# Loading the second query block of a prompt attention with the first, and a sample group's memory scores three side steps later

## The chip, the cores and the metric

The kernel runs on one core of one Trainium2 chip. The metric is the device time of one execution in microseconds; the median of the runs counts. The engines are named as in the profile: PE (TensorE), ACT (ScalarE), DVE (VectorE), POOL (GpSimd), and SP, whose queue issues most of the DMAs.

## What is computed

One layer of a hybrid decoder trunk, for a prompt (1 x 2048 tokens of 1024) and for a sample group (8 sequences of 4 new tokens, each with 8192 past tokens in a paged cache). One projection gives the inputs of four head groups: a convolution module, a pooling mixer, a stick-breaking attention (8 heads of 64) and a cross-attention into 256 memory tokens (4 heads of 128). Every group's output is multiplied by its own gate; all are concatenated, projected with `w_out`, normalised and added to the residual. The two parts that matter here:

```
def sb_block(q, k, v, bias, q_pos, k_pos):              # stick-breaking attention
    z = einsum('nqhd,nkhd->nhqk', q, k) * (64 ** -0.5) + bias
    mask = k_pos < q_pos
    log_1m = where(mask, log_sigmoid(-z), 0.0)
    rc = cumsum(log_1m, axis=3, reverse=True)
    a = exp(where(mask, log_sigmoid(z) + rc - log_1m, -inf))
    return einsum('nhqk,nkhd->nqhd', a, v)

def mem_attend(q, mk, mv):                              # cross-attention into the memory
    s = einsum('nqhd,nmhd->nhqm', q, mk) * (128 ** -0.5)
    return einsum('nhqm,nmhd->nqhd', softmax(s), mv)
```

## The kernel before

The program has three stages that follow each other on the engines.

The first is the projection of prompt and sample tokens, column group by column group. PE runs its products, and beside them the sample group's attention over the paged cache (`sample_all`) advances by steps that a rate sets. When its last step is through, its buffers are closed, the pool `sbr` of the prompt attention is opened in their place, and the first query block is loaded at once (`load(0, 0)`), while the last two column groups of the projection still run. Their results go to scratch in DRAM (`gsd`, `gcd`, `mixd`, `ydw`) through SP's queue.

The second stage is the prompt's stick-breaking attention, `sb_prompt`. It runs over 4 head pairs `hp` and 4 query blocks `qb` of 512 tokens each; within a block over key blocks `kc` from `qb` down to 0, and there over the two heads `hh` and two halves `q2` of the queries. I call one such step a pair, because it treats two tiles of 128 queries, and number the pairs from 1: block (0, 0) has pairs 1 to 4, block (0, 1) has the diagonal pairs 5 to 8 and the full pairs 9 to 12, and block (0, 2) begins with pair 13. `score` multiplies queries (`Q`) and keys (`kT`) into the PSUM tile `S` (two buffers); ACT makes two sigmoids of it, `gam` and `be`; DVE runs a product scan over `gam` into `E`; POOL multiplies `be` by `E`. Some steps later `turn` transposes `be` on PE into `AT` (two PSUM buffers) and copies it to `at`, and `values` multiplies it with `V` into `av`.

At the start of each block the loads of the next one are issued, if they have not been before:

```
            if bi + 1 < len(blocks) and blocks[bi + 1] not in loaded:
                loaded[blocks[bi + 1]] = load(*blocks[bi + 1])
```

A load of a block is eight DMAs, four of keys and four of queries (two heads, two halves of the partitions); the first block of a head pair also loads the values `V`. There are buffers for four `Q` tiles, two blocks.

Beside the attention a generator of side work, `side_work`, advances by one step each time the attention's cost has grown by `PACE` (4.0), from the ninth of its own steps on (`SLATE`). A full pair costs 2.66, a diagonal one 1.0 or 2.33. The side work is, in order: the sample group's memory attention (`sample_mem`), the rest of its stick-breaking attention (`sample_end`), the first output weights, and, once head pair 3 reports its first blocks, the first output parts and the convolution's second half. `sample_mem` loads eight tiles of transposed memory keys (`mkbT`, 512 KB each), then in two halves multiplies four of them with the sample queries into `smS`, which takes one of the two `AT` buffers, and adds them up in `smsc` on DVE. After each half it loads four tiles of memory values (`mvb`) into the key tiles' buffers. Then come the maximum `smx` on DVE, the exponential `smp` on ACT, which needs another activation table than the sigmoids, transposes, products with the values (`smO`) and the gate.

The third stage multiplies the mixed groups with `w_out` and normalises.

The order of PE's instructions is the order in which the code issues them. The other engines' orders, SP's queue among them, are set by a scheduler from the program; each engine then works through its own order, waiting where it must.

Of the kernel before, what the change touches and what calls it, by code (L numbers as in the profile page):

```python
# [37 lines left out]
K4 = 4  # L38
PACE = 4.0
SLATE = 8  # L40
LEAD = 2
LPACE = 3
AHEAD = 4
# [43 lines left out]
def kernel(  # L87
# [1043 lines left out]
    def sample_mem(sm, ps_, S):  # L1131
# [18 lines left out]
        def load(b):  # L1150
            t = sm.tile([P, 2, 512], F32, tag="mkb", name=f"mvb{b}", bufs=8)
            sp.dma_start(t, cmv[b].rearrange("(t p) c -> p t c", p=P))
            return t

        kT = []
        for b in range(NB):
            kT.append(sm.tile([P, 4, NMEM], F32, tag="mkb", name=f"mkbT{b}", bufs=8))
            sp.dma_start(kT[b], mkTd[b])
        vb = {}
        for k in range(2):  # L1160
            yield
            S = ps_(f"smS{k}")
            for b in range(4 * k, 4 * k + 4):
                for h in range(4):
                    pe.matmul(S[32 * h : 32 * h + 32, :NMEM], lhsT=qm[:, b, h, :], rhs=kT[b][:, h, :], start=b == 4 * k,
                              stop=b == 4 * k + 3, tile_position=(0, 32 * h))
            if k:
                dve.tensor_tensor(out=sc, in0=sc, in1=S[:, :NMEM], op=ALU.add)
            else:
                dve.tensor_copy(sc, S[:, :NMEM])  # L1170
            for b in range(4 * k, 4 * k + 4):
                vb[b] = load(b)
# [52 lines left out]
    def sb_loader(sbr):  # L1225

        KT, V = {}, {}

        def load(hp, qb):
            tok = slice(512 * qb, 512 * qb + 512)  # L1230
            Q = []
            for hh in range(2):
                pr = slice(64 * hh, 64 * hh + 64)
                kt = sbr.tile([P, 512], F32R, tag="kT", name=f"kT{hp}_{qb}_{hh}", bufs=10)
                qt_ = sbr.tile([P, 2, 512], F32R, tag="Q", name=f"Q{hp}_{qb}_{hh}", bufs=4)
                for x in range(2):
                    hx = slice(64 * x, 64 * x + 64)
                    sp.dma_start(kt[hx].bitcast(F32), kd[hp, pr, x, tok])
                    sp.dma_start(qt_[hx].bitcast(F32), qd[hp, pr, :, tok])
                KT[hp, hh, qb] = kt  # L1240
                Q.append(qt_)
            if qb == 0:
                V[hp] = sbr.tile([P, 16, P], F32, tag="V", name=f"V{hp}", bufs=2)
                sp.dma_start(V[hp], vd[:, P * hp : P * (hp + 1)].rearrange("(t p) c -> p t c", p=P))
            return Q, KT, V[hp]

        return load
# [336 lines left out]
    def out_weights(prod, pool_, eng, lead=1, raw=lambda j: "opm", lag=1):  # L1584


        ts = {}
        for j in range(lead):
            if j:
                yield  # L1590
            ts[j] = weight_load(prod, j, raw(j))
        for j in range(8 + lag):
            yield
            if 0 < j < 9:
                weight_high(prod, j - 1, ts[j - 1], pool_)
            if j >= lag:
                weight_low(prod, j - lag, ts.pop(j - lag), eng)
            if j < 8:
                weight_sum(prod, j, ts[j])
            if j + lead < 8:  # L1600
                ts[j + lead] = weight_load(prod, j + lead, raw(j + lead))
# [63 lines left out]
    def out_high(x):  # L1665
        prod, i, h = x
        rows = P if i < LAST else NS
        mh, ml = [opm.tile([P, 4, P], F32R, tag=n, name=f"{n}{prod}_{i}_{h}", bufs=2 * LEAD) for n in ("mh", "ml")]
        act.copy(mh[:, :, :rows], raws[x])  # L1669
# [145 lines left out]
    def main():  # L1815
        yield from z_groups(0, GROUPS[0][4:12])
        tasks.add(later_stats())
        yield from z_groups(0, GROUPS[0][12:14])
        tasks.add(sample_keys())
        yield from z_groups(0, GROUPS[0][14:])  # L1820
        tasks.add(state_rows(0))
        yield from z_groups(1, GROUPS[1][:-2])
        tasks.add(state_rows(1))
        yield from z_groups(1, GROUPS[1][-2:])
# [4 lines left out]
    due, blk = 0.0, {}  # L1829
    sbr = bx = None  # L1830
    for cost in main():
        tasks.step()
        due += rate * cost
        while sample is not None and due >= 1.0:
            due -= 1.0
            try:
                next(sample)
            except StopIteration:
                sample = None
                sx.close()  # L1840
                bx = ExitStack()
                sbr = bx.enter_context(tc.tile_pool(name="sbr", bufs=1, side="right", reuse_waits="tile"))
                load = sb_loader(sbr)
                blk[0, 0] = load(0, 0)
    tasks.drain()
    zx.close()

# [20 lines left out]
    last_ *= 2  # L1868
    lead_ = parts[: 2 * LEAD]
    raws, mix, accs, keep, stores = {}, {}, {}, {}, []  # L1870
# [3 lines left out]
    def side_work():  # L1874
        nonlocal opm, conv
        for i, part in enumerate((sample_mem, sample_end)):
            with tc.tile_pool(name=f"sm{i}", bufs=1, side="left", reuse_waits="tile") as sm2:
                yield from part(sm2, side_ps, S)
        opm = ox.enter_context(tc.tile_pool(name="opm", bufs=1, side="left", reuse_waits="tile"))
        yield from out_weights(1, opm, pool)  # L1880
        while (3, 0) not in flags:
            yield
        for x in lead_:
            out_load(x)
            out_combine(x)
            out_high(x)
            out_low(x, pool)
            yield

        while (3, 1) not in flags:  # L1890
            yield
        for x in parts[2 * LEAD : 2 * LEAD + 3]:
            out_load(x)
        cp = cx.enter_context(tc.tile_pool(name="cp", bufs=1, side="left", reuse_waits="tile"))
        conv = conv_post(cp, lambda n: conv_ps[0](n), lambda: cx.enter_context(
            tc.tile_pool(name="cpw", bufs=1, side="left", reuse_waits="tile")))
        while "centered" not in flags:
            next(conv)
            yield
# [30 lines left out]
    for cost in sb_prompt(load, blk, sb, bps, ops, flags):  # L1930
        steps += 1
        if steps > SLATE:
            due += cost
# [31 lines left out]
    def weights_after():  # L1965
# [4 lines left out]
        def spread(gen, start, step):  # L1970
            yield start
            for k, _ in enumerate(gen):
                yield start + step * k

        yield 2 * LEAD
        wr = lambda j: "wr"
        yield from spread(out_weights(7, op, dve, 1, wr), 2 * LEAD, 1.5)
        yield from spread(out_weights(2, opm, dve, 2, wr), at((7, 0, 0)) + 1, 1.4)
# [49 lines left out]

    ready = {d: set(lead_ if d < 3 else parts[: 2 * LEAD + 3]) for d in (3, 1, 0, -1)}
    for n, x in enumerate(parts):  # L2030
# [64 lines left out]
```

## Time and profile before

| | us |
|---|---|
| median of 3 runs | 2420.67 |
| the runs | 2415.16, 2420.67, 2429.53 |
| the profiled execution | 2418.47 |
| its span, first to last instruction | 2416.7 |
| PE busy in it | 2285.6 (95%) |
| DVE, POOL, ACT busy | 1718.3, 1306.8, 1117.5 |
| projection ends (last product begins) | 1490.28 |
| first product of the prompt attention | 1492.15 |
| first and last load of queries issued | 1475.53, 1874.9 |

Times within the profile count from the start of the span. A row of an engine gives the start, the time that the group of instructions took, and in brackets how long the engine had been idle and what ended that. The granted clock is that of TensorE, 1.00 being full speed.

### The profile page before, as it was taken

What the parts mean: (1) busy time and instruction counts of PE and PEld (TensorE: products, weight loads), DVE (VectorE), ACT (ScalarE), POOL (GpSimd) and SP (SyncE); (2) the same over time, 40 slices, a digit from 0 to 9 for tenths busy, and PEclk for the clock granted to TensorE, in tenths of its full rate; (3) what the DMA queues carried; (4) which work ended last, traced back from release to release, by engine and by line L of the source; (5) the groups of instructions that cost most, each with busy time, mean ns of one, the idle gap of its engine ahead of it and who ended that gap; (6) DMA issues with size and microseconds to landing.
All of it is one profiled execution on the core that took longest, in us unless ns stands there. A gap on an engine that the chain in (4) does not pass through costs nothing. (4 is left out here: it accounts for less than half of the span.)

```text
span 2416.7 us, 42137 instructions
## 1 busy us (share of the span) xinstructions
PE 2285.6 (95%) x15962; PEld 1774.5 (73%) x15962; DVE 1718.3 (71%) x2410; ACT 1117.5 (46%) x1939; POOL 1306.8 (54%) x1333
## 2 busy tenths in 40 slices
PE   7999999999999999999999998899999998989897
PEld 6998978898888777777777776455555556768775
DVE  5333774959757664587877777879798846687998
ACT  5322343242442322124242434788989954443554
POOL 2554544556574555655556564667877755453430
PEclk9999999999999999999999999999999999999998
DMA  5789988887778899987887767834333227887764
GB/s 179 223 260 298 348 290 287 284 272 263 263 254 292 277 344 325 323 287 262 275 270 269 262 218 179 239 79 117 89 88 79 64 64 242 266 272 254 245 234 170
DMA packets 340437, 562.14 MB, mean 233 GB/s; under 512 B 28481, under 2 KB 212929, under 8 KB 323834
## 3 DMA queue, kind: packets, MB, share of 16 engines
q1 hardware_dynamic: 284858, 290.72, 39.2%
q0 software_dynamic: 55376, 268.72, 31.3%
q8 instruction: 126, 2.06, 0.3%
q14 instruction: 77, 0.63, 0.1%
HBM read 469.28 MB, written 90.68 MB: 232 GB/s over the span
## 5 line engine op out<-in xcount | busy, mean ns | idle before, releaser
L959 DVE STREAM_TRANSPOSE T<-kt 128x1024 f32<-128x1024 f32 x256 | 308.9, 1226 | 183.4 <-PE sSA L972 177.2
L926 POOL DMA_INDIRECT vt<-in_cache_v_dram,idv x256 | 251.6, 983 | 242.1 <-PE sO L1011 181.5
L617 DVE SCALAR_TENSOR_TENSOR cacc<-U,par,cacc 128x512 f32<-128x512 f32 x480 | 360.2, 750 | 11.8
L1311 POOL TENSOR_TENSOR be<-be,E 128x512 f32<-128x512 f32 (+2 forms) x320 | 303.8, 957 | 118.4 <-DVE E L1302 52.4
L1302 DVE TENSOR_TENSOR_SCAN E<-gam,cr,ZM 128x513 f32<-128x513 f32 x192 | 232.8, 1262 | 15.1 <-ACT gam L1287 14.2
L926 POOL DMA_INDIRECT kt<-in_cache_k_dram,idk x128 | 126.2, 986 | 201.9 <-DVE T L959 146.8
L1322 PEld LDWEIGHTS AT<-ident,be 128*128 128x128 f32 x1088 | 117.7, 142 | 127.6 <-ACT at L1328 45.4
L1287 ACT ACTIVATE gam<-S,nbias_bc 128x1024 f32<-128x1024 f32 (+1 forms) x160 | 172.6, 1079 | 50.8 <-ACT be L1289 18.9
L1915 PE MATMUL acc<-wohi,mh 128*128 128x512 f32 (+1 forms) x480 | 193.3, 403 | 0.6 <-ACT mh L1669 0.6
L1915 PE MATMUL acc<-wolo,mh 128*128 128x512 f32 (+1 forms) x480 | 189.6, 395 | 0.0
L1915 PE MATMUL acc<-wohi,ml 128*128 128x512 f32 x448 | 178.1, 398 | 11.6 <-DVE ml L1680 11.6
L1282 PE MATMUL S<-kT,Q 128*128 128x512 f32 (+1 forms) x640 | 177.9, 401 | 6.8 <-DMA Q<-qd 2.7
L1289 ACT ACTIVATE be<-S,bias_bc 128x1024 f32<-128x1024 f32 (+1 forms) x160 | 171.6, 1073 | 0.0
L1322 PE MATMUL AT<-ident,be 128*128 128x128 f32 x1088 | 158.1, 284 | 14.1 <-ACT at L1328 4.2
L1338 PE MATMUL av<-at,V 128*64 128x512 f32 (+3 forms) x640 | 153.0, 557 | 1.7 <-DVE sbo L1343 1.7
L972 PE MATMUL sSA<-T,W 128*32 128x128 f32 x4096 | 139.2, 277 | 6.4 <-DVE T L959 5.6
L972 PEld LDWEIGHTS sSA<-T,W 128*32 128x32 f32 x4096 | 104.7, 110 | 43.6 <-issue 35.3
L1680 DVE TENSOR_TENSOR ml<-mr,mh 128x512 fp32r<-128x512 f32 x108 | 98.1, 914 | 38.4 <-ACT mh L1669 38.2
L1282 PEld LDWEIGHTS S<-kT,Q 128*128 128x128 f32 x640 | 107.1, 195 | 23.0 <-ACT be L1289 3.5
L1011 PE MATMUL sO<-vt,saT 128*32 128x512 f32 x1024 | 122.4, 592 | 0.0
L1299 DVE TENSOR_TENSOR_SCAN E<-gam,ZM 128x128 f32<-128x128 f32 (+3 forms) x128 | 96.4, 802 | 30.1 <-ACT gam L1287 25.2
L1328 ACT COPY at<-AT 128x512 f32<-128x512 f32 x192 | 108.9, 655 | 14.4 <-PE AT L1322 14.4
(571 smaller groups left out, 6043.7 us busy)
## 6 DMA issues: line engine op xcount, KB each, us to landing
Q<-qd SPq DMA_DIRECT2D x64, 256.0 KB
mr<-mixd SPq DMA_DIRECT2D x32, 512.0 KB
mr<-mixd SPq DMA_DIRECT2D x48, 256.0 KB
wor<-in_w_out_dram SPq DMA_DIRECT2D x20, 512.0 KB
xtp<-in_x_prompt_dram SPq DMA_DIRECT2D x16, 512.0 KB
kT<-kd SPq DMA_DIRECT2D x64, 128.0 KB
wor<-in_w_out_dram SPq DMA_DIRECT2D x32, 256.0 KB
msd<-mr SPq DMA_DIRECT2D x32, 256.0 KB
```

Of the source, the lines that this page charges most:

```text
L617: dve.scalar_tensor_tensor(out=ps, in0=U[:, a + k : a + k + H], scalar=wd[:, k : k + 1], in1=ps, op0=ALU.mult, op1=ALU.add)
L926: pool.indirect_dma_start(out=dst, out_offset=None, in_=rows, in_offset=bass.IndirectOffsetOnAxis(ap=idx, axis=0))
L959: dve.transpose(T[:, 2 * hh : 2 * hh + 2].rearrange("p s j t -> p (s j t)"), kt[:, 2 * hh : 2 * hh + 2].rearrange("p s j d -> p (s j d)"))
L972: pe.matmul(sSs[n][32 * g : 32 * g + 32, P * ml : P * (ml + 1)], lhsT=W[:, jj, :], rhs=T[:, :, jj, :], start=i == 0, stop=i == 3, tile_pos ...
L1282: pe.matmul(S[:, j, :w], lhsT=Q[hh][:, x, P * (q2 + j) : P * (q2 + j + 1)], rhs=KT[hp, hh, kc][:, :w], start=x == 0, stop=x == 1)
L1287: act.activation(out=ga[:, :, 512 - w : 512], in_=S[:, :, :w], func=AF.Sigmoid, bias=nbias_bc[:, h : h + 1], scale=-1.0)
L1289: act.activation(out=be[:, :, :w], in_=S[:, :, :w], func=AF.Sigmoid, bias=bias_bc[:, h : h + 1])
L1302: dve.tensor_tensor_scan(out=E[:, j][:, ::-1], data0=ga[:, j][:, ::-1], data1=ZM[:, 0:1].to_broadcast([P, 513]), initial=carry[hh, q2][:, ...
L1311: pool.tensor_tensor(out=be[:, j, :m], in0=be[:, j, :m], in1=E[:, j, 513 - w : 513 - w + m], op=ALU.mult)
L1322: pe.transpose(ap_[:, P * qt : P * (qt + 1)], A[hp, qb, kc, hh, qt][:, P * r : P * (r + 1)], ident)
L1338: pe.matmul(av[64 * hh : 64 * hh + 64, c], lhsT=V[:, 4 * kc + r, 64 * hh : 64 * hh + 64], rhs=ats.pop((hp, qb, kc, r, hh))[:, c], start=dg ...
L1915: pe.matmul(o[:rows], lhsT=m[a][:, k, :rows], rhs=W[prod, 4 * h + k][w], start=not cont and h == k == n == 0, stop=h == 1 and k == 3 and n ...
```

## The change

Two edits. The loads of the second query block, (0, 1), are issued right behind those of the first, when the sample group's attention closes, instead of at the start of the attention; the block is then marked as loaded, so the attention does not load it again. And `sample_mem` takes three more steps between loading the memory keys and its first product.

```
+SMLATE = 3
...
             kT.append(sm.tile([P, 4, NMEM], F32, tag="mkb", name=f"mkbT{b}", bufs=8))
             sp.dma_start(kT[b], mkTd[b])
         vb = {}
+        for _ in range(SMLATE):
+            yield
         for k in range(2):
             yield
             S = ps_(f"smS{k}")
...
                 load = sb_loader(sbr)
                 blk[0, 0] = load(0, 0)
+                blk[0, 1] = load(0, 1)
     tasks.drain()
```

How the orders move. First SP's queue at the end of the projection, before the change (`kT_1_0` is the key tile of block 1, head 0; `gsd`, `gcd`, `mixd` and `ydw` are stores of the projection):

```order
L1244 DMA V_14530<-vd 128x16x128
L716 DMA gsd<-sg1sg_0_14544 128x512
L716 DMA gcd<-sg1cg_1_14584 128x512
L540 DMA mixd<-mo_3_512_14597 128x4x128
L624 DMA ydw<-acc_3_1_14646 128x512
L1238 DMA kT_1_0_14680<-kd 64x512
L716 DMA gsd<-sg1sg_1_14627 128x512
L1239 DMA Q_1_0_14681<-qd 64x2x512
L1238 DMA kT_1_0_14680<-kd 64x512
L1239 DMA Q_1_0_14681<-qd 64x2x512
```

and the same place after it:

```order
L1247 DMA V_14530<-vd 128x16x128
L1241 DMA kT_1_0_14532<-kd 64x512
L1242 DMA Q_1_0_14533<-qd 64x2x512
L1241 DMA kT_1_0_14532<-kd 64x512
L1242 DMA Q_1_0_14533<-qd 64x2x512
L1241 DMA kT_1_1_14538<-kd 64x512
L1242 DMA Q_1_1_14539<-qd 64x2x512
L1241 DMA kT_1_1_14538<-kd 64x512
L1242 DMA Q_1_1_14539<-qd 64x2x512
L717 DMA gsd<-sg1sg_0_14556 128x512
L717 DMA gcd<-sg1cg_1_14596 128x512
L541 DMA mixd<-mo_3_512_14609 128x4x128
```

The eight loads of the second block have moved ahead of the five stores. The loads of the third block and of the memory keys follow behind the stores, as they followed behind the second block's loads before.

Then PE in the second block. The name of `S` holds head pair, query block, key block, head and half. Before:

```order
L1282 MATMUL S0_1_0_0_0_14870<-kT0_0_0_14518,Q0_1_0_14681 128x512 x4
L1338 MATMUL av0_0_14885<-at0_0_0_0_0_14796,V0_14530 64x512
L1338 MATMUL av0_0_14885<-at0_0_0_0_1_14803,V0_14530 64x512
L1322 MATMUL AT0_0_0_2_0_14888<-ident_87,be0_0_0_0_2_14707 128x128 x2
L1322 MATMUL AT0_0_0_2_1_14893<-ident_87,be0_0_0_1_2_14728 128x128 x2
L1165 MATMUL smS0_14898<-mkbT0_14827,qm_14808 32x256 x4
L1165 MATMUL smS0_14898<-mkbT1_14829,qm_14808 32x256 x4
L1165 MATMUL smS0_14898<-mkbT2_14831,qm_14808 32x256 x4
L1165 MATMUL smS0_14898<-mkbT3_14833,qm_14808 32x256 x4
L1282 MATMUL S0_1_0_0_2_14924<-kT0_0_0_14518,Q0_1_0_14681 128x512 x4
```

After, five pairs on, in the third block:

```order
L1285 MATMUL S0_2_2_0_2_15022<-kT0_2_0_14736,Q0_2_0_14737 128x512 x4
L1341 MATMUL av0_1_15009<-at0_1_1_1_0_14974,V0_14530 64x384
L1341 MATMUL av0_1_15009<-at0_1_1_1_1_14980,V0_14530 64x384
L1325 MATMUL AT0_1_1_3_0_15037<-ident_87,be0_1_1_0_2_14768 128x128
L1325 MATMUL AT0_1_1_3_1_15041<-ident_87,be0_1_1_1_2_14848 128x128
L1168 MATMUL smS0_15045<-mkbT0_14827,qm_14808 32x256 x4
L1168 MATMUL smS0_15045<-mkbT1_14829,qm_14808 32x256 x4
L1168 MATMUL smS0_15045<-mkbT2_14831,qm_14808 32x256 x4
L1168 MATMUL smS0_15045<-mkbT3_14833,qm_14808 32x256 x4
L1285 MATMUL S0_2_2_1_0_15071<-kT0_2_1_14742,Q0_2_1_14743 128x256 x4
```

The first half of the memory scores stood between pairs 9 and 10; it now stands behind pair 14. The second half moves from behind pair 11 to behind pair 17.

Last ACT around the exponential `smp` of the memory scores, before:

```order
L1289 ACTIVATE be0_1_0_1_0_14954<-S0_1_0_1_0_14949,bias_bc_118 128x1024
L1178 ACT_TABLE_LOAD
L1178 ACTIVATE smp_14991,sms_14992<-smsc_14826,smx_14988 128x256
L1287 ACT_TABLE_LOAD
L1287 ACTIVATE gam2_14678<-S0_1_0_1_2_15012,nbias_bc_119 128x2x512
```

and after:

```order
L1331 COPY at0_1_0_2_0_15189<-AT0_1_0_2_0_15184 128x512
L1181 ACT_TABLE_LOAD
L1181 ACTIVATE smp_15177,sms_15178<-smsc_14826,smx_15174 128x256
L1331 COPY at0_1_0_2_1_15196<-AT0_1_0_2_1_15191 128x512
L1290 ACT_TABLE_LOAD
L1290 ACTIVATE gam2_14690<-S0_2_1_0_2_15198,nbias_bc_119 128x2x512
```

The exponential has moved from between two pairs of the second block to between two copies of transposed weights in the third. From the time at which side work waits for head pair 3, the orders of all engines are the same as before.

More of the change, by code (lines that the diff above doesn't have):

```diff
@@ L40 @@
 SLATE = 8
+SMLATE = 3
 LEAD = 2
@@ L1159, in sample_mem @@
         vb = {}
+        for _ in range(SMLATE):
+            yield
         for k in range(2):
@@ L1844 @@
                 blk[0, 0] = load(0, 0)
+                blk[0, 1] = load(0, 1)
     tasks.drain()
```

## The prediction

> **What bounds the kernel now.** The change touches one place, so I read the page's head first, then the rows around that place: what each engine waited for, the instructions of TensorE (PE), ScalarE (ACT), VectorE (DVE) and of the DMA queue in order of time, and last the busy time by stretch.
>
> ```profile
> span 2416.7 us, 42137 instructions
> PE 2285.6 (95%) x15962; PEld 1774.5 (73%) x15962; DVE 1718.3 (71%) x2410; ACT 1117.5 (46%) x1939; POOL 1306.8 (54%) x1333
> ```
>
> PE is busy for 95% of the span. What can be won is in the few places where it is not, and the prompt attention's first 40 us, from 1490 on, are one. The waits of 1490 to 1545 (engine, line and tile that waited, for whom, total us, times, longest):
>
> ```profile
> ACT gam L1287 <- issue: 10.4, 2, 8.2
> PE smS L1165 <- DMA mkbT<-mkTd: 3.5, 4, 2.1
> PE S L1282 <- DMA Q<-qd: 2.7, 2, 1.7
> ```
>
> These are the two waits that the change speaks of: the sample group's memory scores (smS) for their transposed keys (mkbT), and the second query block's scores (S) for its queries (Q). PE in order of time (start, us, operation, and in brackets the idle time before it and what ended it):
>
> ```profile
> 1496.84 1.19 PE L1282 MATMUL S<-kT,Q 128*128 128x512 f32 x4 [1.79 <-ACT be L1289]
> 1499.71 2.90 PE L1282 MATMUL S<-kT,Q 128*128 128x256 f32 x8 [1.68 <-DMA Q<-qd]
> 1503.67 1.19 PE L1282 MATMUL S<-kT,Q 128*128 128x256 f32 x4 [1.05 <-DMA Q<-qd]
> ...
> 1511.06 0.65 PE L1322 MATMUL AT<-ident,be 128*128 128x128 f32 x4
> 1513.79 0.64 PE L1165 MATMUL smS<-mkbT,qm 128*32 128x256 f32 x8 [2.08 <-DMA mkbT<-mkTd]
> ...
> 1517.55 1.08 PE L1165 MATMUL smS<-mkbT,qm 128*32 128x256 f32 x8 [0.20 <-DMA mkbT<-mkTd]
> 1518.56 2.08 PE L1282 MATMUL S<-kT,Q 128*128 128x512 f32 x4
> ...
> 1523.45 1.93 PE L1165 MATMUL smS<-mkbT,qm 128*32 128x256 f32 x32
> ```
>
> PE runs its instructions in the order written. It is done with the transposes at 1511.71 and could score the next pair, but stands from there to 1518.56 on the first half of smS. ACT and DVE starve behind it:
>
> ```profile
> 1500.99 0.69 ACT L1287 ACTIVATE gam<-S,nbias_bc 128x512 f32<-128x512 f32 x1 [0.76 <-ACT be L1289]
> 1502.70 1.12 ACT L1287 ACTIVATE gam<-S,nbias_bc 128x1024 f32<-128x1024 f32 x1 [0.44 <-ACT be L1289]
> 1508.36 1.12 ACT L1287 ACTIVATE gam<-S,nbias_bc 128x1024 f32<-128x1024 f32 x1 [2.15 <-issue]
> ...
> 1511.37 1.12 ACT L1289 ACTIVATE be<-S,bias_bc 128x1024 f32<-128x1024 f32 x1
> 1520.73 1.12 ACT L1287 ACTIVATE gam<-S,nbias_bc 128x1024 f32<-128x1024 f32 x1 [8.23 <-issue]
> ```
>
> ```profile
> 1513.34 2.45 DVE L1302 TENSOR_TENSOR_SCAN E<-gam,cr,ZM 128x513 f32<-128x513 f32 x2
> 1518.70 0.42 DVE L1170 COPY smsc<-smS 128x256 f32<-128x256 f32 x1 [2.92 <-PE smS L1165]
> 1522.52 0.49 DVE L1326 TENSOR_TENSOR at<-AT,tri 128x128 f32<-128x128 f32 x2 [3.40 <-PE AT L1322]
> 1522.93 4.79 DVE L1302 TENSOR_TENSOR_SCAN E<-gam,cr,ZM 128x513 f32<-128x513 f32 x4
> ```
>
> ACT has no work from 1512.49 to 1520.73. DVE ends a scan at 1515.79 and starts the next scan at 1522.93, with 0.42 + 0.49 us of work between. By stretch (length, then busy us of PE, PEld, DVE, ACT, POOL, then granted clock, DMA share, GB/s):
>
> ```profile
> 1490.70:1497.90 7.20, 3.45 (x16) 2.35 (x16) 3.78 (x6) 5.51 (x8) 3.64 (x10) 1.00 0.70 184
> 1497.90:1508.40 10.50, 7.77 (x27) 6.29 (x27) 7.27 (x10) 6.85 (x10) 7.20 (x11) 0.52 1.07 220
> 1515.80:1522.90 7.10, 6.43 (x28) 2.63 (x29) 0.80 (x3) 2.12 (x2) 1.14 (x2) 0.54 1.03 400
> 1522.90:1536.00 13.10, 11.17 (x87) 6.35 (x85) 12.05 (x20) 10.00 (x12) 5.45 (x6) 1.00 0.57 185
> 1536.00:1545.00 9.00, 8.57 (x53) 5.30 (x52) 7.68 (x12) 8.66 (x13) 7.59 (x15) 1.00 1.05 290
> 1545.00:1648.00 103.00, 95.98 (x554) 54.06 (x552) 88.04 (x113) 86.65 (x113) 70.89 (x101) 1.00 0.49 117
> 1648.00:1660.00 12.00, 10.41 (x54) 7.21 (x54) 9.98 (x21) 4.12 (x6) 4.61 (x5) 0.72 0.38 95
> ```
>
> From 1515.8 to 1522.9 PE looks busy, but at a clock of 0.54, with DVE at 0.80 us and ACT at 2.12 us of 7.10. After it DVE is the limit (12.05 of 13.10), and from 1536 on PE and ACT are (8.57 and 8.66 of 9.00).
>
> **The early load.** It adds and removes no instruction: eight loads of the second block move in the queue of SP ahead of the projection's last five stores.
>
> ```profile
> 1480.05 0.54 SPq L1244 DMA_DIRECT2D V<-vd  x1
> 1480.68 4.57 SPq L716 DMA_DIRECT2D gsd<-sg1sg  x1
> ...
> 1490.30 0.32 SPq L624 DMA_DIRECT2D ydw<-acc  x1
> 1490.67 0.46 SPq L1238 DMA_DIRECT2D kT<-kd  x1
> ```
>
> Today the eight stand behind ydw, which waits for its data until 1490.30. After the change they follow V. The issue behind V takes 4.57 us; that now falls to the first key load, and the eight at 0.5 to 0.6 us each (the 0.46 and 0.54 of these rows) end at about 1490. The stores go some 5 to 7 us later. Nobody is near them: their readers are the gate tiles of the attention, which multiply only at the end of a block, and the convolution stage. Cost 0; if that cover were gone it would be those 5 to 7 us.
>
> The DMA engines move the same bytes. Between 1490.7 and 1497.9 their share is 0.70, so 0.30 x 7.20 = 2.2 us of idle transfer time is filled, and everything behind lands about 2.2 us sooner. Today the eight are issued from 1490.67 on and let PE start 9.0 us (first head, 1499.71) and 13.0 us later (second head, 1503.67). Counted from 1485.25, where the 4.57 ends, that is 1494.3 and 1498.3; PE could use them from 1498.03 (1496.84 + 1.19) and 1502.6 (1503.67 - 1.05). Both Q waits go. On ACT, which sets the pace there, these waits show as 0.76 + 0.44 = 1.2 us; that is the term I take. Lower end 0 (DVE, itself at 7.27 of 10.50, may be late next); upper end 1.2 + 2.15 = 3.3, if the idle time at 1508.36 goes too. That one is not a wait for data: PE works from 1503.67 on without a gap, at half clock.
>
> On that clock the Trainium skill has a rule ("TensorE: Matmul & The Clock Gate", Part 1): the clock halves after an idle window of about 3.4 us. This trace differs: the longest gap before the half-clock stretch is 1.79 us, and PE is merely 3.45 us busy in 7.20. By the rule no stretch of the changed kernel would be at half clock and the term would be 3.3; by the row it is 1.2, since 1490.7 to 1497.9 is paced by ACT (5.51 of 7.20) before any Q wait and stays as it is.
>
> **The later scores.** A side step comes after every 4.0 of attention cost, a full pair costs 2.66 and the two diagonal pairs in between 1.0 and 2.33. Three steps are 12, and the first smS goes behind five more pairs (10 to 14): 3 x 2.66 + 1.0 + 2.33 = 11.3.
>
> Removed. With smS gone from 1513.79, PE scores pair 10 at 1511.71; four matmuls at full clock take 1.19 us (the row at 1496.84), so ACT starts at 1512.9 instead of 1520.73 (7.8 us sooner) and is done by 1515.1 (1.12 + 1.11). DVE, the later one, ends its scan at 1515.79, does the 0.49 and starts the next scan at 1516.3 instead of 1522.93: 6.6 us. That is the term; ends 6.3 (DVE's idle time, 7.10 - 0.80) and 8.2 (ACT's). The keys are there when smS comes: the first half's last pair of matmuls found them at 1517.55, now about 1515.3; ACT alone needs 3 x 2.23 + 1.37 + 2.23 = 10.3 us for five pairs from 1512.9, so smS is not reached before about 1521 and waits for nothing.
>
> Added. The same side work now falls into full stretches. Rows of it as it runs now:
>
> ```profile
> 1525.75 1.28 ACT L1178 ACT_TABLE_LOAD   x1
> 1527.64 0.39 DVE L1168 TENSOR_TENSOR smsc<-smsc,smS 128x256 f32<-128x256 f32 x1
> ...
> 1528.71 0.51 ACT L1178 ACTIVATE smp<-smsc,smx 128x256 f32<-128x256 f32 x1 [1.68 <-DVE smx L1175]
> 1529.13 0.19 ACT L1178 ACTIVATION_READ_ACCUMULATOR smp<-smsc,smx 128x1 f32 x1
> 1529.81 1.28 ACT L1287 ACT_TABLE_LOAD   x1 [0.50 <-PE S L1282]
> ```
>
> PE: 1.93 us for each half, 3.9 in all, of which the second half was partly paid before. ACT: 1.28 + 0.51 + 0.19 + 1.28 = 3.3 us, plus a wait like the 1.68, which lay in a stretch where ACT had room (10.00 of 13.10) and come to one where it has little (8.66 of 9.00). smS also holds one of two transpose banks until DVE has copied it out, now behind scans. DVE gets 0.39 us and more back where it was the limit. Behind the ACT instruction that waits for smx stand a copy that PE's av needs, and two activations. Ends: below nothing by the 0.4 on DVE, up to 3.9 + 3.3 + 1.7 = 8.9 if nothing overlaps. I take 2.5: 1545 to 1648 leaves ACT 16 us in 103 to catch up and PE 7, so most of ACT's part is absorbed, and PE's first half (1.9) and a little of the rest are not. The rest of the side chain comes three steps later too and then waits for the end of a head pair, as now: 0 behind it.
>
> **Sum.** 6.6 + 1.2 - 2.5 = 5.3 us. The profiled execution took 2418.47 us (span 2416.7): 2413.2. The median of the three timed runs, 2420.67, is 2.2 above it: 2415.4, so I say 2415 us, 0.2% less. About 0.5%, 12.1 us, is what a measurement of this kernel can tell from no change: its runs alone span 14 us.
>
> **Rivals.** *The moved work costs more than the stall (slower).* Place: pairs 14 to 20, in the third query block, where ACT stands in front of smx with DVE's scans ahead of it, and PE starves. Price: 8.9 us as above, and a half-clock stretch like 1515.8 to 1522.9, where 6.43 us of PE at 0.54 would be 3.5 at full clock: 2.9. Together 11.8 against 7.8 won: 4.0 slower, 2422.5 by the profiled execution, 2425 by the median. It decides from 7.8 us of unabsorbed loss on. For it: ACT's 8.66 of 9.00. Against: the 16 us of room just behind.
>
> *More goes than the stall.* The sample group's last steps run at 1648 to 1660 at a clock of 0.72. PE there:
>
> ```profile
> 1648.81 1.91 PE L1113 MATMUL nyn<-nanT,vsn 32*64 32x32 f32 x16 [1.99 <-DVE at L1326]
> ```
>
> They move by three steps against the block's diagonal. If they then meet a less loaded DVE, 10.41 us at 0.72 become 7.5 (2.9 less), and the 1.99 goes: 4.9 more, 10.2 in all, 2408.3, by the median 2410. Against: the move can as well find a worse place, so I count it at 0 in the sum.
>
> *The clock stays up from the first block on.* The term of the early load is then 3.3 instead of 1.2, the gain 7.4: 2411.1, by the median 2413. For it: two of the waits inside the stretch go. Against: the stretch begins before them. This is where the page's rule leads.
>
> **How the numbers follow.** Forecast (gain 2 to 7) 0.57, slower rival 0.18, more goes 0.14, clock 0.11. The forecast's own range is 2413 to 2419. For 8 in 10 the range must take in most of both outer rivals and the few us by which a median of runs moves: 2406 to 2425. Faster by over 0.5% (under 2408.6) needs the second rival and some luck: 0.14. Slower by over 0.5% (over 2432.8) needs nearly twice the price of the first: 0.06. Within: 0.80.
>
> **What would show it.** Right: no DMA wait before S or smS; the second scan of the second block's first full pairs without the idle time from 1515.8; ACT's longest gap before 1530 under 2 us; the attention's end some 5 us earlier, with the last stage as long as now. Wrong: smS still waiting for mkbT (then the transfers were not sooner); a gap of ACT or PE of over 5 us around the moved smp; a half-clock stretch after 1530; or a change in the output stage, for which I have no reason.

## The result, and the profile after

The changed kernel takes 2428.49 us (median of 22 runs, 2423.19 to 2439.94), the kernel before 2422.55 in the same rounds (22 runs, 2415.16 to 2430.28): a ratio of 1.0028, 95% interval 1.0018 to 1.0037. The two medians are 5.9 us apart; the ratio on record is not exactly their quotient (1.0025) and makes it 6.8 us (0.0028 x 2422.55). Either way the change is slower, by less than 0.5%, and outside the range. The profiled execution took 2424.25 us.

The head of the page of the changed kernel:

```profile
span 2422.6 us, 42146 instructions
PE 2288.1 (94%) x15962; PEld 1774.9 (73%) x15962; DVE 1718.3 (71%) x2410; ACT 1118.2 (46%) x1939; POOL 1303.6 (54%) x1333
```

The span is 5.9 us longer, the work the same. To place the difference I use the sigmoid `gam`, of which each pair has one: its start, counted from the first pair's, against the same in the kernel before. First and last of the 160 in the kernel before, and then in the changed one (ACT in order of time):

```profile
1492.99 0.69 ACT L1287 ACTIVATE gam<-S,nbias_bc 128x512 f32<-128x512 f32 x1 [1.62 <-PE S L1282]
...
1952.87 1.10 ACT L1287 ACTIVATE gam<-S,nbias_bc 128x1024 f32<-128x1024 f32 x1
```

```profile
1496.00 0.69 ACT L1290 ACTIVATE gam<-S,nbias_bc 128x512 f32<-128x512 f32 x1 [1.61 <-PE S L1285]
...
1961.17 1.10 ACT L1290 ACTIVATE gam<-S,nbias_bc 128x1024 f32<-128x1024 f32 x1
```

From first to last are 459.88 and 465.17 us: the attention is 5.3 longer. The 3.0 us by which it starts later is not the change: the first key load, ahead of the change's place, is already 3.0 later. On the way the difference is +2.9 at pair 3, -11.6 at pair 13, +0.8 at pair 19, -2.3 at 35, +2.6 at 37, -2.2 at 53, +6.0 at 61, and about that to the end. So the forecast gain is there at pair 13, and more; 2.9 us were lost ahead of it, and 12.4 are lost from pair 13 to 19. From there to pair 53 gains and losses (-4.5 from 19 to 24, +4.9 from 35 to 37, -4.8 from 37 to 53) leave 3.0 us gained: side steps that stand at other pairs now cost there and are saved where they stood. Then 8.2 are lost from pair 53 to 61.

**Ahead: pairs 1 to 3.** The waits of the changed kernel from 1490 to 1545:

```profile
ACT gam L1290 <- PE S L1285: 9.1, 4, 5.3
DVE E L1302 <- DMA ydw<-acc: 8.5, 1, 8.5
...
PE S L1285 <- ACT be L1292: 6.6, 3, 4.7
...
ACT be L1292 <- DMA gcd<-sg1cg: 2.8, 1, 2.8
...
PE smS L1168 <- DVE at L1329: 2.2, 1, 2.2
```

No Q wait and no mkbT wait is left, as forecast. In their place DVE's first scan (`E`) waits 8.5 us, and ACT's `be` 2.8, for two stores of the projection to land. Neither reads what is stored. `E` and `be` are tiles of a pool that opens when the projection's pools are closed; as I read it, they lie on the memory of the tiles `acc` and `sg1cg`, which the stores must have left; no run shows the addresses. SP's queue says why the stores are late. Its first key load of the kernel before, then the rows of the changed one:

```profile
1474.78 0.53 SPq L1238 DMA_DIRECT2D kT<-kd  x1
```

```profile
1477.80 0.53 SPq L1241 DMA_DIRECT2D kT<-kd  x1
...
1483.64 5.29 SPq L1241 DMA_DIRECT2D kT<-kd  x1
...
1494.21 0.41 SPq L717 DMA_DIRECT2D gsd<-sg1sg  x1
1495.23 0.34 SPq L717 DMA_DIRECT2D gcd<-sg1cg  x1
...
1497.63 0.32 SPq L625 DMA_DIRECT2D ydw<-acc  x1
```

The early load's first issue takes 5.29 us behind V. Counted from the first key load, `gsd` is issued by 16.8 us (1494.62 - 1477.80; before, 1485.25 - 1474.78 = 10.5) and `ydw` at 19.8 (before, 1490.30 - 1474.78 = 15.5): 6.3 and 4.3 us later, and behind them on the way are the eight loads.

**Pairs 13 to 19.** PE and then ACT of the changed kernel around the moved scores:

```profile
1531.56 3.21 PE L1168 MATMUL smS<-mkbT,qm 128*32 128x256 f32 x32 [2.22 <-DVE at L1329]
1534.70 1.07 PE L1285 MATMUL S<-kT,Q 128*128 128x256 f32 x4
```

```profile
1535.86 0.69 ACT L1290 ACTIVATE gam<-S,nbias_bc 128x512 f32<-128x512 f32 x1 [5.31 <-PE S L1285]
...
1545.27 1.28 ACT L1181 ACT_TABLE_LOAD   x1
1546.56 0.51 ACT L1181 ACTIVATE smp<-smsc,smx 128x256 f32<-128x256 f32 x1
...
1547.65 1.28 ACT L1290 ACT_TABLE_LOAD   x1
1548.95 1.12 ACT L1290 ACTIVATE gam<-S,nbias_bc 128x1024 f32<-128x1024 f32 x1
```

By stretch (length, busy us of PE, PEld, DVE, ACT, POOL, clock, DMA share, GB/s):

```profile
1511.40:1529.30 17.90, 16.26 (x86) 9.20 (x84) 17.90 (x28) 13.74 (x15) 11.98 (x16) 0.99 0.71 261
1529.30:1535.80 6.50, 4.28 (x39) 2.27 (x40) 5.69 (x9) 1.25 (x2) 5.48 (x9) 0.74 0.99 220
```

Before the scores DVE has no idle time at all (17.90 of 17.90). The scores need a transpose buffer that DVE empties behind its scans; PE waits 2.22 us for it, runs at a clock of 0.74 and starves ACT for 5.31 us. The two table loads, with the exponential 3.3 us, then stand in a full row of sigmoids.

**Pairs 53 to 61.** DVE, PE and ACT of the changed kernel at the end of the sixth block, (1, 1):

```profile
1653.79 1.25 DVE L1329 TENSOR_TENSOR at<-AT,tri 128x512 f32<-128x512 f32 x2
1657.71 0.48 DVE L1108 TENSOR_SCALAR nrb<-ident,ngc 128x128 f32<-128x128 f32 x2 [2.67 <-DMA ngc<-gnd]
1658.11 0.68 DVE L1346 TENSOR_TENSOR sbo<-av,sgt 128x512 f32<-128x512 f32 x1
```

```profile
1658.85 1.98 PE L1341 MATMUL av<-at,V 128*64 128x512 f32 x4 [2.73 <-DVE sbo L1346]
```

```profile
1662.89 1.12 ACT L1290 ACTIVATE gam<-S,nbias_bc 128x1024 f32<-128x1024 f32 x1 [5.13 <-PE S L1285]
```

A side operation, `nrb`, stands on DVE until a small tile of the sample group (`ngc`) has come back from DRAM. Behind it is the block's output `sbo`, for which PE's next `av` waits, and behind that ACT. In the kernel before the same `nrb` waits longer, but elsewhere (DVE):

```profile
1631.45 0.48 DVE L1107 TENSOR_SCALAR nrb<-ident,ngc 128x128 f32<-128x128 f32 x2 [5.00 <-DMA ngc<-gnd]
```

There ACT goes on as if nothing waited: pairs 43 to 47, around this wait, take 10.6 us, and pairs 83 to 87, the same place of the next head pair, 10.9.

### The profile page after: what moved, and what is told of

Same layout as the page of the kernel before. It is cut to its first block, busy times and chain, and to the rows that moved or that the text cites. A ratio compares the mean times of both kernels' runs of the same rounds, so it can differ in the third digit from the quotient of the medians.

```text
span 2422.6 us, 42146 instructions
## 1 busy us (share of the span) xinstructions
PE 2288.1 (94%) x15962; PEld 1774.9 (73%) x15962; DVE 1718.3 (71%) x2410; ACT 1118.2 (46%) x1939; POOL 1303.6 (54%) x1333
## 5 line engine op out<-in xcount | busy, mean ns | idle before, releaser
L1919 PE MATMUL acc<-wohi,ml 128*128 128x512 f32 x448 | 178.6, 399 | 11.1 <-DVE ml L1683 10.9
```

The source lines that it names most:

```text
L1919: pe.matmul(o[:rows], lhsT=m[a][:, k, :rows], rhs=W[prod, 4 * h + k][w], start=not cont and h == k == n == 0, stop=h == 1 and k == 3 and n ...
```

## The experiments

Theory: the change is a sum of parts of both signs. The local move of scores and exponential gains; the rest of the sample group's chain, which comes three steps later with them, costs; the early load costs through the stores. Rival: what is lost is the price of scores and exponential at their new place, as the slower rival of the prediction had it.

In the table, "attention" is the first to last `gam` against the 459.88 us of the kernel before, from one profiled execution each; ratios are those on record, against the kernel before run beside it (the quotients of the medians differ from them by up to 0.0010).

| kernel | ratio (95%) | attention, us |
|---|---|---|
| the change | 1.0028 (1.0018, 1.0037) | +5.3 |
| the change again | 1.0026 (1.0013, 1.0040) | +3.1 |
| early load alone | 0.9993 (0.9978, 1.0007) | -3.5 |
| later scores alone, with all behind them | 1.0005 (0.9992, 1.0018) | +0.9 |
| local move: the rest left in its place | 0.9983 (0.9970, 0.9995) | -5.8 |
| the rest alone three steps later | 1.0026 (1.0011, 1.0040) | +6.8 |
| early load and local move | 1.0006 (0.9991, 1.0021) | -3.6 |
| the same, early load by POOL | 0.9998 (0.9986, 1.0010) | -3.4 |
| local move by 1 step | 0.9977 (0.9965, 0.9988) | -7.2 |
| local move by 2 steps | 1.0004 (0.9991, 1.0017) | -3.7 |
| the change, last stores by POOL | 1.0030 (1.0020, 1.0040) | +0.6 |
| early load, 1 step, last stores by POOL | 1.0010 (0.9996, 1.0024) | -2.7 |
| 1 step, the rest 2 steps earlier | 1.0017 (1.0004, 1.0029) | -1.4 |
| last stores by POOL alone | 0.9987 (0.9976, 0.9999) | -6.4 |
| early load, local move, last stores by POOL | 0.9986 (0.9974, 0.9997) | -2.2 |
| the change, `nrb` moved | 1.0018 (1.0003, 1.0033) | +0.2 |
| local move by 1 step, `nrb` moved | 0.9986 (0.9977, 0.9995) | -6.8 |
| kernel before, `nrb` moved | 1.0001 (0.9989, 1.0012) | -0.6 |

### The two edits apart

```
early load alone:         + blk[0, 1] = load(0, 1)
later scores alone:       + SMLATE = 3, as in the change
```

> Only the early load; the memory scores stand where they stood before. Theory: the loss of the change comes from the place of the later side steps, and the early load by itself is small: it puts the waits of the attention's first tiles for the projection's stores in (pairs 3 to 9 about 2.9 us late, as in the changed kernel), and the memory keys come some 2 us sooner, so the stall on them at pair 10 is shorter; from pair 13 on -1 to +3 us against before, whole time within 3 us of before. Rival A, the early load is what costs: 5 to 6 us slower than before, as the change, with the delay of 2.9 us never made up. Rival B, the change's gain of 14 us between pairs 9 and 13 comes from the early load: pair 13 about 10 us earlier here too.

> Only the three later steps; the second block is loaded where it was before. Theory: no waits for stores at pairs 3 to 9; the stall on the memory keys goes (pair 13 about 11 to 14 us earlier than before, counted from pair 1); smS and smp then cost 10 to 13 us between pairs 14 and 18, and the rest of the side work, three steps later, another 4 to 7 up to pair 60; 2 to 6 us slower than before in all. Rival A, the early load is what costs: no loss here, 5 us or more faster than before. Rival C, the keys still come late: a wait of smS for mkbT at its new place.

Both came out better than expected, 3.5 us shorter and 0.9 longer in the attention. Neither alone is a measured loss (0.9993 and 1.0005), and together they are 1.0028. The store waits come with the early load; DVE and then PE of the kernel with the early load alone:

```profile
1502.42 7.53 DVE L1299 TENSOR_TENSOR_SCAN E<-gam,ZM 128x128 f32<-128x128 f32 x11 [8.32 <-DMA ydw<-acc]
```

```profile
1516.40 1.76 PE L1165 MATMUL smS<-mkbT,qm 128*32 128x256 f32 x24 [2.14 <-DVE at L1326]
1518.81 0.64 PE L1165 MATMUL smS<-mkbT,qm 128*32 128x256 f32 x8 [0.64 <-DMA mkbT<-mkTd]
```

Its attention is 2.8 us behind at pair 3, 0.4 behind at pair 9 and 2.9 ahead at pair 11. It makes up 2.4 us where the waits for Q were, and 3.3 at the scores. Their wait for mkbT goes from 3.5 us to 0.6, but 2.14 of the rest is now a wait for the transpose buffer, so PE's idle time there falls only from 3.5 to 2.8. The clock does more: it is 1.00 from 1513.5 to 1520.5, where the kernel before has 0.54 from 1515.8 to 1522.9, and the next pair's products take 1.20 us in place of 2.08. The later scores take the same stall away: the two edits are paid once for it.

### The chain split

In `sample_mem` six empty steps stand between the exponential and the transposes. Shortened to three, they leave all that follows at its step; lengthened to nine, with the scores in their place, they move only what follows.

```
local move:               + SMLATE = 3;   6 -> 3 yields behind smp
the rest alone later:                     6 -> 9 yields behind smp
early load + local move:  + blk[0, 1] = load(0, 1); SMLATE = 3; 6 -> 3 yields
```

> The three later steps ahead of the memory scores, and three of the six empty steps behind the exponential taken out, so that everything from the transposes smpt on stands at the same side step as before; no early load. Theory: what is won up to pair 13 (11 to 14 us) and lost at pairs 14 to 18 (10 to 13) is as in the kernel with the later steps alone, and the later loss up to pair 60 (4 to 7 us) is gone: within 3 us of before. Rival D, the place of smS and smp is all that costs, and the rest of the chain is neutral: the same time as with the three later steps alone, 2 to 6 us slower than before.

> Before, with nine empty steps instead of six behind the exponential: memory scores at their old place with their old stall, everything from smpt on three steps later; no early load. Theory: pairs 1 to 24 as before, then a loss of 4 to 7 us against before up to pair 60, where the sample group's last steps meet another part of the blocks; 4 to 7 us slower. Rival D, the rest of the chain is neutral: within 2 us of before at every pair.

> As the kernel before it, but with the early load on SP as in the change. Theory: pairs 3 to 9 about 2.9 us late by the waits for the stores, and no stall on the keys left behind which that could hide, so 3 to 4.5 us longer than the local move alone; against before 1 to 3 us shorter. Rival A3 (the early load is worth 3 us whatever stands behind it, as when it was made alone): 9 us shorter than before.

The local move is faster, by more than expected in the attention: 0.9983, or 4.1 us (0.0017 x 2419). The rest alone costs 6.3 us (0.0026 x 2419). The same part is taken out twice more: later scores alone against the local move (1.0005 - 0.9983) and the change against early load and local move (1.0028 - 1.0006), 0.0022 or 5.3 us both times. So the cost of the rest is 5 to 6 us by the ratios in three pairs of kernels, and 6.6 to 8.9 in the attention. By the widths of the intervals, I estimate that a difference of two ratios is good to about 0.002, 5 us. A fourth pair, with the last stores on POOL (below), has the sign but not the size: 0.0044 by the ratios (1.0030 - 0.9986), 10.6 us, and 2.8 in the attention. The early load on top of the local move is 0.0023, or 5.6 us by the ratios, but 2.2 in the attention.

Where a step of the rest meets scans, in the kernel with it alone later: PE, then DVE in front of it, at pair 35.

```profile
1599.87 1.09 PE L1325 MATMUL AT<-ident,be 128*128 128x128 f32 x4 [2.40 <-DVE smOm L1210]
```

```profile
1594.35 4.79 DVE L1305 TENSOR_TENSOR_SCAN E<-gam,cr,ZM 128x513 f32<-128x513 f32 x4
1599.06 0.67 DVE L1210 TENSOR_TENSOR smOm<-smO,hm 128x512 f32<-128x512 f32 x1
```

The second product with the values (`smO`) holds a transpose buffer until DVE has passed four scans. From pair 35 to 37 this kernel loses 5.0 us against the kernel before. But the loss does not stay there: at pair 53 it is 4.3 us ahead (1.0 of that already at pair 13), as it saves the same steps where they stood, and from there to pair 61 it loses 11.3. The later scores against the local move say the same: 0.2 ahead at pair 53, 6.8 behind at 61. So what the rest costs, it costs from pair 53 on. DVE, PE and ACT of the kernel with the rest alone later, at the end of the sixth block:

```profile
1654.15 0.48 DVE L1107 TENSOR_SCALAR nrb<-ident,ngc 128x128 f32<-128x128 f32 x2 [3.27 <-DMA ngc<-gnd]
```

```profile
1655.29 1.98 PE L1341 MATMUL av<-at,V 128*64 128x512 f32 x4 [3.32 <-DVE sbo L1346]
```

```profile
1660.10 1.12 ACT L1290 ACTIVATE gam<-S,nbias_bc 128x1024 f32<-128x1024 f32 x1 [6.79 <-PE S L1285]
```

It is the chain of the changed kernel, without early load and without later scores.

### Is it the wait for ngc?

```
-   two nrb multiplications right behind the load of ngc, then 6 yields
+   6 yields, then the two nrb multiplications, then nyn
```

> The changed kernel with the two nrb operations moved behind six empty steps, to just before their product is needed. If DVE's wait for ngc with sbo behind it is what pairs 53 to 61 pay: they lose less than 4 us against the kernel before instead of 7 to 8, the attention ends 3 to 5 us sooner than in the changed kernel (0 against before), ratio about 1.001. If the side work at this place costs by itself: pairs 53 to 61 lose 7 us as they did, ratio 1.0025 to 1.003.

> The kernel before with the two nrb operations behind the six empty steps. DVE's wait of 5.0 us for ngc goes. If it is covered (PE runs on through it in the trace, fed by ACT): attention within 1 us of before, ratio 0.9995 to 1.0005. If it costs: -3 to -5 us, ratio 0.998.

> The shortest kernel so far (scores one step later, rest of the chain in its place, no early load) with the two nrb operations behind the six empty steps. If the wait for ngc (5.0 us, in the fourth block) is covered there: as short as without, -7 us in the attention, ratio 0.9977. If it costs: 3 to 5 us shorter still, 0.996.

With `nrb` moved in the changed kernel, DVE goes from `at` to `sbo` at once:

```profile
1651.80 1.25 DVE L1328 TENSOR_TENSOR at<-AT,tri 128x512 f32<-128x512 f32 x2
1652.97 0.67 DVE L1345 TENSOR_TENSOR sbo<-av,sgt 128x512 f32<-128x512 f32 x1
```

Pairs 53 to 55, which cost 2.8 and 3.0 us in the two profiles of the change, gain 0.4. Pairs 53 to 61 still lose 5.1 (8.3 and 6.9 without the edit). So the wait is 2 to 3 us of it. The other 5 I put down to side work at this place (`nyn`, `nys`, `nym`); no run took that away. By the ratios the edit is 1.0018 against 1.0028 and 1.0026: a step that way, with overlapping intervals. In the kernel before the same edit does nothing (1.0001), but it tests nothing either. The scheduler left `nrb` where it was in DVE's order, and DVE still waits (DVE of the kernel before with `nrb` moved):

```profile
1641.74 0.48 DVE L1109 TENSOR_SCALAR nrb<-ident,ngc 128x128 f32<-128x128 f32 x2 [4.48 <-DMA ngc<-gnd]
```

With one step and `nrb` moved it waits 4.2 us, so 0.9986 against 0.9977 says nothing of the wait either. That the 5.00 us of the kernel before are covered rests on ACT's steps there alone (10.6 and 10.9 us, above).

### Whose are the store waits?

```
early load by POOL:       load(0, 1) through pool.dma_start, SMLATE = 3, 3 yields
last stores by POOL:      gsd, gcd, ydw, mixd of the last groups through pool.dma_start
```

> Second block loaded early, but its eight loads are issued by POOL instead of SP, so the projection's stores keep their place in SP's queue; memory scores three steps later, the rest of the side work at its old step (three of the six empty steps taken out). Theory (the early load costs because the attention's first tiles E and be lie on the buffers of stores that it pushes back): no wait of E for ydw nor of be for gcd, the waits for Q gone, pairs 5 to 9 about 1 us earlier than before, and the attention as long as with the local move alone or 1 us shorter: 5 to 7 us shorter than before. Rival A2 (the loss is the transfers themselves, competing with V and the stores): pairs 3 to 9 some 3 us late as with the load on SP, 3 to 5 us lost against the local move alone.

> The whole change, and the projection's last stores (gsd, gcd, ydw, mixd), those issued after the early load, go out from the queue of POOL instead of SP's. Theory (the early load costs what the delayed stores cost: the first tiles be and E of the attention lie on memory that these stores still read): the waits of DVE for ydw (8.5 us) and of ACT for gcd (2.8) fall to under 2 us each, pair 3 starts within 0.5 us of where it starts in the kernel before (now 2.9 later), and the attention ends some 4 us sooner than in the changed kernel, about +1 us against before. Rival (the early load's own transfers, or the shift of all that follows, is the cost): the waits may go, and the attention still ends 5 us later than before.

> The kernel before with the projection's last stores on POOL's queue, nothing else changed. If these stores on POOL cost time outside the attention: a ratio of 1.002 to 1.003 with the attention within 1 us of before. If they cost nothing: a ratio within 0.9995 to 1.0005.

> Scores three steps later, the rest of their chain in its place, early load, last stores on POOL's queue. If the delayed stores are all that the early load costs: the attention as short as with the local move alone (-5.8 us), against -3.6 with the early load and the stores on SP. If the early load costs by itself: -3.6 again.

This line did not settle, and none of the four came out wholly as expected. Issued by POOL, the early load still blocks SP:

```profile
1492.22 10.02 SPq L716 DMA_DIRECT2D gsd<-sg1sg  x1
```

And with the stores on POOL `E` still waits, 6.4 us (POOL, then DVE of the change with the last stores by POOL):

```profile
1491.86 0.54 POOL L625 DMA_DIRECT2D ydw<-acc  x1 [2.71 <-ACT acc L624]
```

```profile
1499.77 6.69 DVE L1302 TENSOR_TENSOR_SCAN E<-gam,ZM 128x128 f32<-128x128 f32 x10 [6.38 <-ACT be L1292]
```

The row names `be`, but `ydw` took 7.8 us from its issue to its landing, so it landed at 1499.7, when `E` started. In the kernel with the local move and the same stores the same first scan waits 6.0 us for `ydw` by its row:

```profile
1504.11 6.15 DVE L1299 TENSOR_TENSOR_SCAN E<-gam,ZM 128x128 f32<-128x128 f32 x9 [6.02 <-DMA ydw<-acc]
```

Counted from the first key load, POOL issued `ydw` at 15.8 us (1491.86 - 1476.07), as SP did in the kernel before (15.5). There `E` started 4.5 us after the issue (1494.77 - 1490.30) and did not wait for `ydw`. So what is late here is the landing and not the issue. The eight loads are ahead of the store in both kernels, as the rival of the transfers has it, but POOL's queue may be slower too: in the change, with the store on SP, `E` started 6.0 us after the issue (1503.64 - 1497.63). No run parts the two.

So the edit did not take away the wait that it was to take away; pair 3 is 1.7 us late instead of 2.9. The attention of the change came back to +0.6, but its ratio did not (1.0030); with the local move the ratio fell by 0.0020 and the attention grew by 1.4. That the early load costs on top of the later scores is measured; that the whole of it is the store waits is not shown. What did gain was unforeseen: the kernel before with its last stores on POOL, where the second block's loads no longer stand behind the stores: 0.9987, attention 6.4 shorter, and no mkbT wait.

### How far to move

> Memory scores one step later instead of three, behind pair 11; the rest of the side work at its old step; no early load. Theory: PE comes to smS at about 1517, when the first half's keys have just landed (1517.55 before), and DVE has fewer scans queued than at three steps; most of the stall goes (8 to 13 us won up to pair 13) and the loss behind is smaller than at three steps (5 to 8 us instead of 10): 3 to 9 us shorter than before. Rival C2 (the keys set it): still 3 us or more of waits for mkbT, and less won than with three steps.

> Memory scores two steps later, behind pair 12; the rest at its old step; no early load. Theory: the keys are there, 12 to 14 us won up to pair 13; smS still waits for its PSUM buffer behind DVE's scans; 4 to 8 us shorter than before. Rival D2 (it does not matter where in the full stretch smS and smp fall): the same as with three steps, 5.8 us shorter within 1 us.

> Scores one step later, and the rest of the sample group's chain two steps earlier than in the kernel before (no early load). Theory (the steps before the block's end, where the chain stands in the kernel before, are a good place by chance, and any move of them meets scans): 2 to 6 us longer than the same kernel with the rest left in its place (-7.2 in the attention), from pairs 25 to 61 on. Rival (only later costs, because the chain then runs into the output stage's work): as short as that one or shorter.

> Early load, scores one step later with the rest of their chain left at its step, and the last stores from the queue of POOL. If the two gains add: the local move by one step gave -7.2 us in the attention and the early load alone -3.5 with its store waits; so -7 to -11 us, a ratio of about 0.996. If the early load only takes away what the later scores no longer need (they are clear of its Q waits): -7, as the local move alone.

One step has the best ratio, which three steps (0.9983) are not told apart from. Two steps (1.0004, 3.7 us shorter in the attention) fell short of what I expected and are worse than one: with two, the last of the keys are late (2.5 us, the last eight products of the first half); with one, the keys are late by little. PE with two steps, then with one:

```profile
1527.94 1.08 PE L1167 MATMUL smS<-mkbT,qm 128*32 128x256 f32 x8 [2.53 <-DMA mkbT<-mkTd]
```

```profile
1517.48 1.07 PE L1167 MATMUL smS<-mkbT,qm 128*32 128x256 f32 x16 [1.27 <-DVE at L1327]
1518.80 0.64 PE L1167 MATMUL smS<-mkbT,qm 128*32 128x256 f32 x8 [0.24 <-DMA mkbT<-mkTd]
1520.08 0.64 PE L1167 MATMUL smS<-mkbT,qm 128*32 128x256 f32 x8 [0.64 <-DMA mkbT<-mkTd]
```

The keys are late with two steps because SP's order has changed too. A load of gates (`sgt`), which waits 11.0 us for `sbo` of the block before, stands between the third and the fourth of the eight keys (SP with two steps; with one, all eight are issued in one row at 1507.42):

```profile
1509.52 2.10 SPq L1158 DMA_DIRECT2D mkbT<-mkTd  x3
1523.42 0.32 SPq L1359 DMA_DIRECT2D sgt<-gsd  x1
1523.78 2.50 SPq L1158 DMA_DIRECT2D mkbT<-mkTd  x5
```

With three steps and no early load the order is the same, but the scores come later and find their keys.

With one step the exponential's table loads stand between pairs 13 and 14 and 3.0 us are lost there (-7.4 and -4.4); with three, between pairs 17 and 18, 4.7 (-8.2 and -3.5). ACT with one step:

```profile
1528.66 0.69 ACT L1288 ACTIVATE gam<-S,nbias_bc 128x512 f32<-128x512 f32 x1 [2.11 <-issue]
...
1529.95 1.28 ACT L1180 ACT_TABLE_LOAD   x1
...
1533.16 1.12 ACT L1288 ACTIVATE gam<-S,nbias_bc 128x1024 f32<-128x1024 f32 x1
```

The early load with the stores by POOL on top of the one step was expected to add its gain and adds nothing but loss (1.0010 against 0.9977). Moving the rest two steps earlier costs too (1.0017 against 0.9977): the step at which the kernel before has it is a good one, in both directions. The best kernel, one step with the rest in place, is 0.9977, and 0.9986 with the `nrb` edit on top: by the ratios 3 to 6 us faster than the kernel before, and 10 to 12 faster than the change.

### How sure the places are

> The changed kernel unaltered, a second profiled execution. If the places of gain and loss are a matter of the program: the starts of the pairs lie within 1 us of the first profile's, -12 at pair 13, +5 at the end of the attention, and a ratio of 1.002 to 1.004. If they are a matter of one execution: other places, and the end anywhere from -3 to +5.

The second profile has the same course (+2.4 at pair 3, -12.1 at 13, +0.2 at 19, -3.2 at 53, +3.7 at 61), but ends 2.2 us lower. Most of that comes from pair 57 to 61, where the first profile loses 5.2 us and the second 3.6; the clock there is 0.57 from 1675.0 to 1679.0 in the first, and 1.00 from 1680.0 to 1684.5 in the second. The prompt attention's length in one profile is therefore good to about 2 us, and a ratio to about 3. Ratios and attention differ by up to 6.6 us (the change with stores by POOL: 7.2 by the ratio, 0.6 by the attention); projection and output stage vary by some us from profile to profile, and what of that belongs to a kernel is open.

## Why the prediction was wrong, by its own steps

- *Both Q waits go; no DMA wait before smS.* Right. But the Q waits are not a fixed 2.7 us: with the second block's loads where they were, PE waits 0.6 with the rest alone later, 0.4 and 0.5 with the later scores. These kernels are 0.8 us ahead at pair 9 without any early load. There was less than 1.2 to win. Nor was the stall at the scores a wait for the keys alone: with the keys there earlier, PE waits 2.14 us for the transpose buffer (early load alone).
- *The early load: cost 0, nobody is near the stores.* Failed. The size of the delay was right (5 to 7 us said, 6.3 and 4.3 measured), the cover was not there. I looked for readers of the data; what waits is, as I read it, the next user of the memory, 8.5 and 2.8 us, and the attention is 2.9 behind at pair 3. Alone the load earns that back where the waits for Q were and at the scores; on top of the later scores it costs 2 to 4 us in the attention and 5.6 by the ratios. The 2.2 us by which I had the keys land sooner help only scores that wait for them, and the moved ones do not.
- *Removed 6.6, added 2.5.* Net 4.1, and the local move measures 4.1 (0.9983, interval 1.2 to 7.3); the attention says 5.8. That the size held is luck, for its parts did not: up to pair 13 there are 13.3 won in that kernel, and to pair 19 9.8 given back (both also hold the scores and the exponential themselves, which left the one place for the other). The buffer held behind scans and the two table loads, both named, do the giving back.
- *The rest of the side chain three steps later: 0.* Failed, and by the attention it is the largest miss: 5.3 to 6.3 us by the ratios in three pairs of kernels, 6.6 to 8.9 in the attention, and it stays from pair 53 to 61. That it "then waits for the end of a head pair, as now" took the steps for interchangeable. Against the block's diagonal they meet other things: DVE's wait for `ngc` with `sbo` behind it is 2 to 3 us of it, and the other part is not taken apart.
- *Sum.* By the ratios -4.1 (local move), +5.3 (the rest), +5.6 (early load on top) make +6.8, against -5.3 forecast. These are differences along one path from the kernel before to the change, so that they add up is no proof of its own.
- *The slower rival* (4.0 us slower by its sum, chance 0.18) has the sign, and its place gives back what it said, from -11.6 at pair 13 to +0.8 at pair 19. It is not the cause: the kernel with the local move gives back 9.8 there and is faster. *More goes* failed for the point that it named: moved against the diagonal, the last steps found a worse place. *The clock stays up* failed: after the new gap of 4.69 us (PE waiting for `be`) the clock is 0.52 from 1500.9 to 1511.4, and 0.74 around the scores after one of 2.22. The length of the gap does not set it: with the early load alone, after a gap of 4.55 us, the clock is 0.84 from 1501.5 to 1512.0, and with the local move, after one of 1.79, it is 0.51 from 1495.4 to 1505.9. The Trainium skill ("TensorE: Matmul & The Clock Gate", Part 1) puts the idle window that halves the clock at about 3.4 us; the gap of 4.69 us agrees with it, but half clock came after 1.79 as well.

## What to carry to other kernels

A step moved in a chain moves everything behind it: cost each later step at its new place, by what stands behind its wait on that engine. Before delaying a store, ask who takes over its memory, not only who reads its data. Two edits that remove the same wait are paid for once; run each alone, and the chain cut in two, before adding them up.

## Not expected of the hardware

When POOL issued the early load, SP's next store behind V took 10.02 us to issue (4.57 before): a second queue did not free the first. A wait of 5.00 us on DVE shows no delay in ACT's steps in one place, and one of 2.67, taken away, gave 2 to 3 us in another. A store of 256 KB that POOL issued no later than SP had issued it before took 7.8 us to land; before, the scan that waits for it here started 4.5 us after the issue.
